# Sliding-window attention in half blocks of two heads x 64 queries, with its steps spread over more places

## The chip, the cores and the metric

The kernel runs on one core of a Trainium2 chip. A core has TensorE (PE; its weight loads are shown apart as PEld), VectorE (DVE), ScalarE (ACT), GpSimd (POOL) and SyncE (SP, which issues the DMAs). They run side by side and wait for each other through semaphores. The metric is the time of one execution on the device in microseconds (us).

## The reference

Two layers over 1024 positions of width 1024. Each layer mixes tokens, then channels. What the change touches is the windowed attention: 8 query heads of 64, 2 key/value heads (4 query heads share one), blocks of 128 queries that see their own block of keys and the one before, window 128, and a learned sink per head in the softmax.

```python
k_cat = jnp.concatenate([jnp.pad(kb, pad)[:, :-1], kb], axis=2)
v_cat = jnp.concatenate([jnp.pad(vb, pad)[:, :-1], vb], axis=2)
scores = jnp.einsum("bnqkgd,bnskd->bnkgqs", qb, k_cat).astype(jnp.float32)
scores = scores * (HEAD_DIM ** -0.5)
qi = jnp.arange(BLOCK)[:, None]
kj = jnp.arange(2 * BLOCK)[None, :]
diff = qi + BLOCK - kj
valid = (diff[None] >= 0) & (diff[None] < WINDOW) & (key_abs >= 0)
scores = jnp.where(valid[None, :, None, None], scores, NEG_INF)
probs = jax.nn.softmax(jnp.concatenate([scores, sink], axis=-1), axis=-1)[..., :-1]
out = jnp.einsum("bnkgqs,bnskd->bnqkgd", probs.astype(v.dtype), v_cat)
```

A query sees 128 keys; over a block of 128 queries they spread over 256 keys, over 64 queries over 191.

The rest of a layer: an input projection to q, k, v and a pooling branch, an output projection, a gated feed-forward net of inner width 2816, norms with modulation from a second input, and residuals.

## The kernel before

**Precision.** Dense factors are split into a high part, rounded to float32r, and a low rest (`split`, L213: ScalarE writes the high part at L215, VectorE subtracts at L216). A product of two such factors is three matmuls, high x high, high x low, low x high (`mm3`, L254: L255, L258, L259).

**Halves and streams.** The sequence is cut into 2 halves of 512 positions (`NHALF`), each into 4 blocks of 128 (`NT`). The program is written as generators. `run` (L640) drives one dense stream and, after each of its steps, as many steps of side streams as keep them in proportion; the compiler then orders each engine's instructions within what dependences and buffers allow. Half 0's attention runs beside the input projections of half 1 (`dense`, L1397); half 1's beside the output projection of half 0 (`mix_out`, L967, 16 steps, side stream: modulation sums, L289), then beside the pooling branch's projection (10 steps), then beside the first feed-forward products.

**Attention before.** A group is one block and one key/value head with its 4 query heads: 8 groups a half. A group takes four steps: (a) `att_keys` (each second group) and `att_queries`: keys and queries, high and low parts stacked, are transposed by TensorE (L774, L798) and copied by ScalarE (L784, L787, L803); (b) `att_softmax` of the group before; (c) and (d), for two heads each, `att_scores` (L813, L814: four matmuls with 256 keys; L816: scaling, mask and row maximum on VectorE), then the value products of the pair transposed in the step before, then `att_probs`: four transposes of probabilities (L851) and their split into `pth` and `ph`. In softmax, L835 is the exponential and L841 and L843 scale three rows on VectorE and one on ScalarE. `att_values` makes six matmuls of 256 columns per pair (current and previous block), whose stationary operand holds the 64 value columns of one head and 64 of zeros; all groups of a block add up in the one PSUM bank `pv`, which L879 copies out.

**Buffers.** A tag has a fixed number of buffers in rotation (L100 to L106); a tile that is asked for when all are in use waits for the oldest one's last reader. `msc` is three PSUM banks that attention, transposes and modulation share; `acc` is four banks of the dense products. The biased projections go to `qkv` (L696, L707): 4 tiles a half, 6 buffers.

## Time and profile before

| | us |
|---|---|
| median of 3 runs | 1915.66 |
| lowest, highest | 1914.08, 1919.38 |
| the profiled execution | 1912.51 |
| its span, first to last instruction | 1910.7 |

Granted TensorE clock: 0.997. A row of the groups reads: line, engine, operation, what it writes and reads, shapes (partitions x elements), count | busy us, mean ns of one | idle time of the engine just before, and who ended it. A row of the windows gives, for each engine, the busy time within the stretch and the count. A row of the timeline gives start, duration, engine, line and operation; neighbours of one kind are merged into one row with a count. [...]

### The profile page before, as it was taken

What the parts mean: (1) busy time and instruction counts of PE and PEld (TensorE: products, weight loads), DVE (VectorE), ACT (ScalarE), POOL (GpSimd) and SP (SyncE); (2) the same over time, 40 slices, a digit from 0 to 9 for tenths busy, and PEclk for the clock granted to TensorE, in tenths of its full rate; (3) what the DMA queues carried; (4) which work ended last, traced back from release to release, by engine and by line L of the source; (5) the groups of instructions that cost most, each with busy time, mean ns of one, the idle gap of its engine ahead of it and who ended that gap; (6) DMA issues with size and microseconds to landing.
All of it is one profiled execution on the core that took longest, in us unless ns stands there. A gap on an engine that the chain in (4) does not pass through costs nothing.

```text
span 1910.7 us, 26084 instructions
## 1 busy us (share of the span) xinstructions
PE 1866.3 (98%) x8978; PEld 1539.2 (81%) x8978; DVE 1545.1 (81%) x2898; ACT 950.5 (50%) x1789; POOL 26.8 (1%) x84
## 2 busy tenths in 40 slices
PE   6999999999999999999999989999999999999997
PEld 4887788888888888888888868888888887888886
DVE  5999886668898888788879998846889888877687
ACT  4876795653222223445548667845622222244452
POOL 1000000000000000000000000000000000000000
PEclk9999999999999999999999999999999999999999
DMA  9355563555655665944554464536654565574342
GB/s 324 115 155 153 163 226 122 186 177 183 204 179 189 208 207 178 323 137 145 183 168 128 133 183 165 177 110 208 215 188 150 198 209 202 197 252 150 115 152 102
DMA packets 227428, 341.86 MB, mean 179 GB/s; under 512 B 16952, under 2 KB 124360, under 8 KB 227296
## 3 DMA queue, kind: packets, MB, share of 16 engines
q1 hardware_dynamic: 227152, 340.17, 54.2%
q8 instruction: 70, 1.15, 0.2%
q14 instruction: 62, 0.51, 0.1%
q0 software_dynamic: 32, 0.00, 0.0%
q10 hardware_dynamic: 112, 0.04, 0.0%
HBM read 267.25 MB, written 72.89 MB: 178 GB/s over the span
## 4 chain that ended last, share of the span: by engine, by line
PE 79%; DVE 11%; DMA 5%; ACT 3%; issue 1%; SPq 0%; DVEq 0%; ACTq 0%
PE acc L255 24%; PE acc L258 24%; PE acc L259 24%; DMA ar<-in_ada_w_dram 2%; DVE lo L216 2%; DVE ada L289 2%; PE msc L851 1%; PE msc L519 1%; ACT hi L215 1%; DMA raw<-in_w_up_dram 1%; PE pv L255 1%; DVE ph L216 1%; DMA ar<-x 1%; DVE sb L816 1%; PE pv L258 1%
## 5 line engine op out<-in xcount | busy, mean ns | idle before, releaser
L215 ACT ACTIVATE hi<-raw 128x1024 fp32r<-128x1024 f32 (+1 forms) x388 | 332.4, 869 | 365.8 <-PE acc L258 196.2
L216 DVE TENSOR_TENSOR lo<-raw,hi 128x1024 fp32r<-128x1024 f32 (+1 forms) x388 | 380.0, 986 | 123.6 <-ACT hi L215 122.8
L255 PE MATMUL acc<-t,hi 128*128 128x512 f32 x704 | 274.6, 390 | 1.5 <-ACT hi L215 1.5
L258 PE MATMUL acc<-t,hi 128*128 128x512 f32 x704 | 274.0, 389 | 0.0
L259 PE MATMUL acc<-t,lo 128*128 128x512 f32 x704 | 271.9, 389 | 0.0
L255 PE MATMUL acc<-bh,hi 128*128 128x512 f32 x520 | 202.8, 390 | 0.0
L259 PE MATMUL acc<-bh,lo 128*128 128x512 f32 x520 | 202.4, 389 | 0.0
L255 PE MATMUL acc<-hT,hi 128*128 128x512 f32 x480 | 189.7, 395 | 0.6 <-DVE fn L638 0.6
L258 PE MATMUL acc<-hT,hi 128*128 128x512 f32 x480 | 188.4, 392 | 0.0
L259 PE MATMUL acc<-hT,lo 128*128 128x512 f32 x480 | 187.7, 392 | 0.0
L1107 DVE TENSOR_TENSOR fn<-acc,fn 128x512 f32<-128x512 f32 x220 | 150.2, 683 | 37.4 <-PE acc L259 37.4
L255 PEld LDWEIGHTS acc<-t,hi 128*128 128x128 f32 x704 | 132.2, 188 | 30.8 <-ACT hi L215 3.9
L259 PEld LDWEIGHTS acc<-t,lo 128*128 128x128 f32 x704 | 132.2, 188 | 29.0 <-DVE lo L216 1.5
L258 PEld LDWEIGHTS acc<-t,hi 128*128 128x128 f32 x704 | 132.2, 188 | 27.2
L258 PE MATMUL acc<-ph,hi 128*128 128x512 f32 x320 | 124.6, 389 | 0.0
L1043 ACT ACTIVATE fn<-fn 128x512 f32<-128x512 f32 x44 | 27.8, 633 | 180.3 <-DVE fn L1107 180.3
L289 DVE SCALAR_TENSOR_TENSOR ada<-ar,c_act,ada 128x512 f32<-128x512 f32 x140 | 104.6, 747 | 12.0 <-DMA ar<-in_ada_w_dram 11.0
L259 PEld LDWEIGHTS acc<-bh,lo 128*128 128x128 f32 x520 | 97.6, 188 | 20.4
L255 PEld LDWEIGHTS acc<-bh,hi 128*128 128x128 f32 x520 | 97.6, 188 | 20.0
L255 PEld LDWEIGHTS acc<-hT,hi 128*128 128x128 f32 x480 | 90.2, 188 | 18.9 <-DVE fn L638 1.4
L259 PEld LDWEIGHTS acc<-hT,lo 128*128 128x128 f32 x480 | 90.1, 188 | 18.2
L255 PE MATMUL acc<-hi 128*128 128x512 f32 x256 | 101.1, 400 | 2.8 <-DVE fn L638 1.6
(315 smaller groups left out, 3834.6 us busy)
## 6 DMA issues: line engine op xcount, KB each, us to landing
ar<-in_ada_w_dram SPq DMA_DIRECT2D x160, 256.0 KB
raw<-in_w_gate_dram SPq DMA_DIRECT2D x44, 512.0 KB
raw<-in_w_up_dram SPq DMA_DIRECT2D x44, 512.0 KB
raw<-in_w_in_dram SPq DMA_DIRECT2D x80, 256.0 KB
raw<-keeps SPq DMA_DIRECT2D x40, 512.0 KB
keeps<-fn SPq DMA_DIRECT2D x66, 256.0 KB
two_b<-in_w_down_dram SPq DMA_DIRECT2D x30, 512.0 KB
raw<-keepa SPq DMA_DIRECT2D x25, 512.0 KB
```

The lines of the kernel that those rows point to most:

```text
L215: nc.scalar.activation(hi, src, AF.Copy)
L216: recent["split"] = nc.vector.tensor_sub(lo, src, hi.bitcast(F32))
L255: ins = nc.tensor.matmul(dst, lh, rh, start=first, stop=False)
L258: nc.tensor.matmul(dst, lh, rl, start=False, stop=False)
L259: return nc.tensor.matmul(dst, ll, rh, start=False, stop=last)
L289: ins = nc.vector.scalar_tensor_tensor(acc, w, c_act[:, i : i + 1], acc, op0=ALU.mult, op1=ALU.add)
L519: ins = nc.tensor.transpose(bank[:, t * P : (t + 1) * P], src[t], ident)
L816: nc.vector.tensor_tensor_reduce(out=s[:, ii, :], in0=bank[:, ii * 2 * P : (ii + 1) * 2 * P], in1=mask[:, min(blk, 1), :], scale=SCALE, sc ...
L851: nc.tensor.transpose(bank[:, i * P : (i + 1) * P], s[:, ii, ck * P : (ck + 1) * P], ident)
L1043: nc.scalar.activation(g, g, AF.Silu)
L1107: nc.vector.tensor_add(halves_of(dst)[m], bank, halves_of(src)[m])
```

## The change

Scores are made for two heads x 64 queries in place of one head x 128: 64 queries see 192 keys at most (`SPAN`), so a score product has 192 columns and softmax rows are 192 wide. A group is now (block, r): query half h meets key/value head `h ^ r`, so that each group holds both halves and both heads. The probabilities of a pair lie in 384 columns, cut in three chunks of 128: the first belongs to half 0, the last to half 1, the middle one to both. The outer chunks meet V of the previous and of the current block, the middle one meets `mix`, a tile that takes 64 rows of each. So a group has three value products of three matmuls each in place of four, and six transposes in place of eight. In a layer's first block the absent past is left out. Values are written once per block into two tiles whose zeros are written once per layer (`att_room`).

The steps of a group now lie so: (a) the middle chunk's transposes of group g-2, queries of head 1; (b) keys of the next block, softmax of group g-1; (c) scores, value products of group g-2, V of this block; (d) scores, queries of head 0 of the next block, outer transposes of group g-1. The tail is one group longer (37 steps for 34). `qkv` has 5 buffers, `pth` one of 768 columns in place of two of 512, `qT` two, `vz` two wide ones. Tiles of `uT` and `pt` are given 576 columns, of which the same ones as before are used.

The diff, without the mask's new shape and the renamed widths:

```diff
+UW = 576
+QH = P // 2
+SPAN = P + QH
...
-        mix=dict(cfa=2, cfb=2, qkv=6, bqkv=1, uT=4, pt=2, vz=5, rt=1, qT=1, pth=2, pwh=1, pwl=1),
+        mix=dict(cfa=2, cfb=2, qkv=5, bqkv=1, uT=4, pt=2, vz=2, rt=1, qT=2, pth=1, bd=1, pwh=1, pwl=1),
...
+    def att_room():
+        attn["v"] = [t_("vz", [P, 2, 3, HD], F32R) for _ in range(2)]
+        attn["mix"] = t_("bd", [P, 2, 4, HD], F32R)
+        zero = vz_zero.rearrange("p (a d) -> p a d", a=1)
+        for v in attn["v"]:
+            nc.gpsimd.tensor_copy(v[:, :, 1, :], zero.to_broadcast([P, 2, HD]))
+        for i in range(4):
+            nc.gpsimd.tensor_copy(attn["mix"][:, :, i, :], zero.to_broadcast([P, 2, HD]))
+    def att_vals(blk, qkv):
+        v, mix = attn["v"][blk % 2], attn["mix"]
+        vsrc = qkv[:, QK:QKV].rearrange("p (n d) -> p n d", d=HD)
+        nc.scalar.activation(v[:, 0, 0:3:2, :], vsrc, AF.Copy)
+        nc.vector.tensor_sub(v[:, 1, 0:3:2, :], vsrc, v[:, 0, 0:3:2, :].bitcast(F32))
+        if blk:
+            before = attn["v"][1 - blk % 2]
+            nc.scalar.activation(mix[QH:, :, 0:4:3, :], before[QH:, :, 0:3:2, :].bitcast(F32), AF.Copy)
+        for n in range(NKV):
+            nc.scalar.activation(mix[:QH, :, 2 - n, :], v[:QH, :, 2 * n, :].bitcast(F32), AF.Copy)
     def att_keys(blk, qkv):
...
         stk = part("hi").rearrange("p (n o d) -> p n o d", n=NKV, o=4)
...
                 )
         bv = bank.rearrange("p (n o k) -> p (n o) k", n=NKV, o=2)
         if blk == 0:
...
+            attn["k", 0] = t_("sa", [P, NKV * 2, 2 * P], F32R)
         nc.scalar.activation(attn["k", blk][:, :, P : 2 * P], bv, AF.Copy)
         if blk + 1 < NB:
             nxt = t_("sa", [P, NKV * 2, 2 * P], F32R)
...
                 stk[:, i].rearrange("p a d -> p (a d)"), ident_r,
             )
         qT = t_("qT", [P, GRP * P], F32R)
-        nc.scalar.activation(qT, bank, AF.Copy)
+        nc.scalar.activation(
+            qT.rearrange("p (h i q) -> p h i q", h=2, i=GRP),
+            bank.rearrange("p (i h q) -> p h i q", h=2, i=GRP), AF.Copy,
+        )
         return qT
-    def att_scores(blk, n, u, qT, mx, s):
+    def att_seen(blk, h):
+        return slice((P if h == 0 else QH) if blk == 0 else 0, SPAN)
+    def att_scores(blk, r, u, qTs, mx, s):
         kT = attn["k", blk]
         bank = msc_bank()
...
+        for h in range(2):
+            n, cs = h ^ r, att_seen(blk, h)
+            dst = bank[:, h * SPAN : (h + 1) * SPAN][:, cs]
+            q = qTs[n][:, (2 * h + u) * P : (2 * h + u + 1) * P]
+            for o in range(2):
+                keys = kT[:, 2 * n + o, h * QH : h * QH + SPAN][:, cs]
+                nc.tensor.matmul(dst, q, keys, start=o == 0, stop=o == 1)
+        for h in range(2):
+            cs = att_seen(blk, h)
             nc.vector.tensor_tensor_reduce(
...
+                out=s[:, h * SPAN : (h + 1) * SPAN][:, cs], in0=bank[:, h * SPAN : (h + 1) * SPAN][:, cs],
+                in1=mask[:, cs], scale=SCALE, scalar=-3.0e38, op0=ALU.add, op1=ALU.max,
+                accum_out=mx[:, 2 * h + u : 2 * h + u + 1],
             )
+        if blk == 0:
+            nc.gpsimd.memset(s[:, 0:P], 0.0)
+            nc.gpsimd.memset(s[:, SPAN : SPAN + QH], 0.0)
         return s
-    def att_softmax(n, sts, mx, nsink):
-        hs = slice(n * GRP, (n + 1) * GRP)
+    def att_softmax(blk, r, sts, mx, nsink):
+        hs = slice(2 * r, 2 * r + GRP)
...
+        rows = [
+            sts[i % 2][:, i // 2 * SPAN : (i // 2 + 1) * SPAN][:, att_seen(blk, i // 2)] for i in range(GRP)
+        ]
         for i in range(GRP):
-            sl = sts[i // 2][:, i % 2, :]
-            nc.scalar.activation(sl, sl, AF.Exp, bias=nm[:, i : i + 1], accum_out=sm[:, i : i + 1])
+            nc.scalar.activation(rows[i], rows[i], AF.Exp, bias=nm[:, i : i + 1], accum_out=sm[:, i : i + 1])
         nc.vector.tensor_add(es, es, sm)
         nc.vector.reciprocal(es, es)
         for i in range(GRP):
-            sl = sts[i // 2][:, i % 2, :]
             if i < GRP - 1:
-                nc.vector.tensor_scalar(sl, sl, es[:, i : i + 1], None, op0=ALU.mult)
+                nc.vector.tensor_scalar(rows[i], rows[i], es[:, i : i + 1], None, op0=ALU.mult)
             else:
-                nc.scalar.activation(sl, sl, AF.Copy, scale=es[:, i : i + 1])
-    def att_probs(s):
+                nc.scalar.activation(rows[i], rows[i], AF.Copy, scale=es[:, i : i + 1])
+    def att_probs(blk, sts, ends, probs):
         bank = msc_bank()
...
+        chunks = ([0] if blk else []) + [2] if ends else [1]
+        for i in chunks:
+            for u in range(2):
+                at = (i + u) * P
+                nc.tensor.transpose(bank[:, at : at + P], sts[u][:, i * P : (i + 1) * P], ident)
+        cs = slice(chunks[0] * P, (chunks[-1] + 2) * P)
+        to = slice(0, 2 * P) if not ends else slice(chunks[0] * P, 4 * P)
+        split(*(p[:, to] for p in probs), bank[:, cs])
+    def att_values(blk, r, probs, pmid, cat, t):
+        if r == 0:
             attn["pv"] = ps.tile([P, 512], F32, tag="pv", name="pv", bufs=1)
         pv = attn["pv"]
...
+        v, before = attn["v"][blk % 2], attn["v"][1 - blk % 2]
+        at = 2 * (1 - r)
+        parts = [(before, r, probs, 0)] if blk else []
+        parts += [(v, 1 - r, probs, 2 * P), (attn["mix"], at, pmid, 0)]
+        for k, (src, c, (ph, pl), p0) in enumerate(parts):
+            vh, vl = (src[:, j, c : c + 2, :].rearrange("p a d -> p (a d)") for j in range(2))
+            opening, closing = r == 0 and k == 0, r == 1 and k == len(parts) - 1
             ins = mm3(
...
+                pv[:, r * 2 * P : (r + 1) * 2 * P], vh, vl, ph[:, p0 : p0 + 2 * P], pl[:, p0 : p0 + 2 * P],
+                opening, closing, None if opening else attn["open"],
             )
             if opening:
                 attn["open"] = ins
         if closing:
...
+            for n in range(NKV):
+                ns = slice(n * HD, (n + 1) * HD)
+                for h in range(2):
+                    g = h ^ n
+                    nc.scalar.activation(
+                        cat[ns, :, t * P + h * QH : t * P + (h + 1) * QH],
+                        pv[ns, g * 2 * P : (g + 1) * 2 * P].rearrange("p (j q) -> p j q", j=GRP), AF.Copy,
+                    )
+    ATT_STEPS = NT * 2 * 4 + 4
+    def attention(half, qkvs, nsink, cat):
+        NG = NT * 2
+        prev, late = None, None
+        for g in range(NG + 2):
             cur = None
+            if late:
+                pblk, pr, psts, probs, pmid, pcat, pt = late
+                att_probs(pblk, psts, False, pmid)
             if g < NG:
...
+                t, r = divmod(g, 2)
+                blk = half * NT + t
+                if g == 0:
+                    att_rotary(blk, qkvs[t])
                     att_keys(blk, qkvs[t])
+                    first = att_queries(0, qkvs[t])
+                if r == 0:
+                    qTs = [first, att_queries(1, qkvs[t])]
                     if t + 1 < NT:
                         att_rotary(blk + 1, qkvs[t + 1])
...
+                both = t_("sb", [P, GRP // 2, 2 * SPAN])
+                cur = (blk, t, r, [], t_("st", [P, 8]))
+            if cur or late:
                 yield
+            if cur and r == 1 and t + 1 < NT:
+                att_keys(blk + 1, qkvs[t + 1])
+            nxt = None
             if prev:
-                pblk, pt, pn, sts, mx = prev
-                att_softmax(pn, sts, mx, nsink)
+                pblk, pt, pr, sts, mx = prev
+                att_softmax(pblk, pr, sts, mx, nsink)
+                pth = t_("pth", [P, 3 * 2 * P], F32R)
+                probs = pth[:, : 4 * P], t_("ph", [P, 4 * P], F32R)
+                pmid = pth[:, 4 * P :], t_("ph", [P, 4 * P], F32R)[:, : 2 * P]
+                nxt = pblk, pr, sts, probs, pmid, cat, pt
                 yield
...
+            if cur:
+                cur[3].append(att_scores(blk, r, 0, qTs, cur[4], both[:, 0]))
+            if late:
+                pblk, pr, _, probs, pmid, pcat, pt = late
+                att_values(pblk, pr, probs, pmid, pcat, pt)
+            if cur and r == 1:
+                att_vals(blk, qkvs[t])
+            if cur or late:
                 yield
-            prev = cur
-        flush()
+            if cur:
+                cur[3].append(att_scores(blk, r, 1, qTs, cur[4], both[:, 1]))
+                if r == 1 and t + 1 < NT:
+                    first = att_queries(0, qkvs[t + 1])
+            if nxt:
+                att_probs(nxt[0], nxt[2], True, nxt[3])
+            if cur or nxt:
+                yield
+            prev, late = cur, nxt
...
         bq = t_("bqkv", [P, QKV])
         eng = nc.sync
         eng.dma_start(bq, b_in[l : l + 1, 0:QKV].to_broadcast([P, QKV]))
+        each = t_("st", [P, 8])
+        eng.dma_start(each, sinks[l : l + 1, :].to_broadcast([P, NH]))
         sk = t_("sk", [P, NH])
-        eng.dma_start(sk, sinks[l : l + 1, :].to_broadcast([P, NH]))
-        nc.vector.tensor_scalar(sk, sk, -1.0, None, op0=ALU.mult)
+        for i in range(2):
+            rows = slice(i * QH, (i + 1) * QH)
+            src = each[rows].rearrange("p (m i) -> p m i", i=2)[:, :, i]
+            nc.vector.tensor_scalar(sk[rows, 0:4], src, -1.0, None, op0=ALU.mult)
+            nc.vector.tensor_scalar(sk[rows, 4:6], src[:, 0:2], -1.0, None, op0=ALU.mult)
         d["bq"], d["nsink"] = bq, sk
...
         run(dense0(), 12 if l else 4, (side, 2 if l else 1))
         cats[0] = (t_("cfa", [P, 4, T]), t_("cfa", [P, 4, T]))
         qkvs[1] = [t_("qkv", [P, QKV]) for _ in range(NT)]
+        att_room()
         att = attention(0, qkvs[0], par["nsink"], cats[0][0])
```

92 lines of the change are left out of this document (9 added, 83 removed).

## The prediction

> **What bounds the kernel now.** I read the page first (busy shares), then the windows of the stages in which attention runs, then the timeline for the real pace of TensorE, because the page's busy time is modelled.
>
> ```profile
> span 1910.7 us, 26084 instructions
> PE 1866.3 (98%) x8978; PEld 1539.2 (81%) x8978; DVE 1545.1 (81%) x2898; ACT 950.5 (50%) x1789; POOL 26.8 (1%) x84
> PE 79%; DVE 11%; DMA 5%; ACT 3%; issue 1%; SPq 0%; DVEq 0%; ACTq 0%
> ...
> core 0: us, PE busy (x) PEld busy (x) DVE busy (x) ACT busy (x) POOL busy (x), PEclk, DMA share, GB/s
> 65.00:163.00 98.00, 97.44 (x620) 83.75 (x618) 93.44 (x280) 77.51 (x191) 2.40 (x12) 1.00 0.43 125
> 163.00:201.00 38.00, 33.31 (x166) 24.94 (x165) 36.11 (x92) 23.37 (x56) 0.39 (x2) 1.00 0.65 186
> 201.00:270.00 69.00, 67.12 (x381) 55.53 (x380) 57.63 (x173) 58.19 (x146) 2.89 (x8) 1.00 0.58 194
> 1100.00:1140.00 40.00, 34.52 (x166) 26.10 (x165) 37.04 (x96) 25.14 (x60) 0.00 (x0) 0.97 0.64 182
> ```
>
> The chain is TensorE's for 79%. In layer 0, half 0's attention lies in 65 to 163, half 1's in 163 to 201 (beside the output projection) and 201 to 270. TensorE sets the first and third stretch; in the second VectorE is 95% busy (36.11 of 38) and TensorE waits, as in layer 1's 1100 to 1140 (37.04 of 40). So TensorE work taken out of attention shortens the kernel, provided VectorE loses as much in that second stretch.
>
> The pace of TensorE, from the timeline:
>
> ```profile
> 86.71 0.28 PE L255 MATMUL pv<-pth,vz 128*128 128x256 f32 x1
> 86.83 0.28 PE L258 MATMUL pv<-ph,vz 128*128 128x256 f32 x1
> 86.95 0.28 PE L259 MATMUL pv<-pth,vz 128*128 128x256 f32 x1
> 87.07 0.49 PE L851 MATMUL msc<-ident,sb 128*128 128x128 f32 x3
> 92.86 0.39 PE L255 MATMUL acc<-hT,hi 128*128 128x512 f32 x1
> 93.09 0.39 PE L258 MATMUL acc<-hT,hi 128*128 128x512 f32 x1
> ...
> L851 PE MATMUL msc<-ident,sb 128*128 128x128 f32 x256 | 43.7, 277 | 4.0 <-DVE sb L841 3.0 <-ACT raw L512 0.6 <-DVE st L816 0.3
> 788.18 0.86 PEld L416 LDWEIGHTS msc<-ones_r,ada 128*128 128x128 f32 x7
> L416 PEld LDWEIGHTS msc<-ones_r,ada 128*128 128x128 f32 x32 | 4.2, 191 | 0.3
> L814 PEld LDWEIGHTS msc<-sa,qT 128*128 128x128 f32 x128 | 24.3, 190 | 1.4
> ```
>
> A product of 256 columns lasts 0.28 us but starts 0.12 after the one before it; one of 512 starts 0.23 after. Three probability transposes last 0.49 together, one alone 0.277, so they start 0.11 apart. L416 streams one column, so its seven weight loads show the pace of loading alone: (0.86 - 0.19) / 6 = 0.11 us. The score products' loads last as long (190 ns), so I take 0.11 us as the floor of a product, however few columns it has.
>
> **The change part by part.** There are 16 blocks (8 per layer); 14 are ordinary, and 2 are the first of a layer.
>
> TensorE, per ordinary block. Value products fall from 24 to 18, all still 256 wide: 6 x 0.12 = 0.72 us. Probability transposes fall from 16 to 12: 4 x 0.11 = 0.44. The 16 score products shrink from 256 to 192 columns; with the floor that is 16 x (0.12 - 0.11) = 0.16. Bounds: 0 if a product of 192 keeps the pace of 256, and 0.43 if it shrinks in proportion ((0.23 - 0.12) / 256 = 0.43 ns a column, 64 columns, 16 products); its nearest row is the load floor. Together 1.32 us, 18.5 for 14 blocks. First blocks drop the past: value products 24 to 12 (1.44), transposes 16 to 8 (0.88), scores 0.16, so 2.48, twice 5.0. TensorE loses **23.5 us**. Key and query transposes keep their number.
>
> [...] I follow the trace's load floor.
>
> VectorE and ScalarE:
>
> ```profile
> L816 DVE CUSTOM_DVE_ANT_0 sb<-msc,mask 128x256 f32<-128x256 f32 x128 | 50.4, 416 | 6.0 <-PE msc L814 5.6
> L216 DVE TENSOR_TENSOR ph<-msc,pth 128x512 fp32r<-128x512 f32 x64 | 43.7, 686 | 2.6 <-ACT pth L215 2.0
> L841 DVE TENSOR_SCALAR sb<-sb,st 128x256 f32<-128x256 f32 x45 | 13.2, 347 | 0.2
> L795 DVE TENSOR_TENSOR hi<-qkv,hi 128x256 fp32r<-128x256 f32 x16 | 6.7, 420 | 0.1
> L501 DVE TENSOR_SCALAR cfb<-cfb,rs 128x1024 f32<-128x1024 f32 x2 | 1.4, 745 | 0.0
> L756 DVE TENSOR_TENSOR vz<-qkv,vz 128x64 fp32r<-128x64 f32 x16 | 3.3, 231 | 2.0 <-PE pv L258 2.0
> L835 ACT ACTIVATE sb<-sb,st 128x256 f32<-128x256 f32 x128 | 63.7, 506 | 6.3 <-DVE st L828 6.3
> L215 ACT ACTIVATE pth<-msc 128x512 fp32r<-128x512 f32 x64 | 37.8, 597 | 22.0 <-PE msc L851 21.8
> L794 ACT ACTIVATE hi<-qkv 128x256 fp32r<-128x256 f32 x32 | 13.2, 412 | 5.7 <-PE acc L259 4.9 <-DVE ada L289 0.8
> L755 ACT ACTIVATE vz<-qkv 128x64 fp32r<-128x64 f32 x16 | 3.4, 250 | 6.1 <-DVE qkv L696 4.4 <-PE pv L259 1.7
> L879 ACT ACTIVATE cfa<-pv 128x512 f32<-128x512 f32 x4 | 2.3, 584 | 0.0
> L392 ACT ACTIVATE ar<-msc 4x512 f32<-4x512 f32 x1 | 0.6, 589 | 0.6 <-PE msc L388 0.6
> ```
>
> VectorE's slope is (686 - 420) / 256 = 1.04 ns a column, and (745 - 347) / 768 = 0.52 for the scaling of L841. Per ordinary block: 8 mask reductions shorter by 64 columns, 8 x 66 = 0.53 us; 6 scalings, 0.20; two of four low halves of 512 become 256 wide, 2 x 266 = 0.53; the V low halves become one of two, 231 against some 300 instead of 462, 0.16. That is 1.42, 20 us for 14 blocks and, with narrower rows and no past, some 3 for each first block: about **26 us**. In the VectorE-bound stretch run 16 of half 1's 37 steps (1.7 blocks a layer): VectorE saves 1.42 a block where TensorE would have saved 1.32, so that stretch shortens as much and the 23.5 stands.
>
> ScalarE gains work. Its slope is (597 - 412) / 256 = 0.72 ns a column. One copy of the finished block (584 ns) becomes four of 64 partitions x 256, which cost like 128 x 256, since 4 partitions (L392) cost 589; 4 x 412 - 584 = +1.06 us. The mixed V tile adds one copy of 256 columns and two of 128, 412 + 2 x 300 = +1.01. Less: 8 exponentials x 46, one scaling, two shorter high halves of 185, and one V copy instead of two (0.2): -1.0. Net **+1.1 us a block**, 17 in all. I cost it at nothing: ScalarE is 58.19 of 69 busy even from 201 to 270, where 2.3 blocks bring 2.5 us. If that cover fails it costs up to 2.5 a layer.
>
> GpSimd loses the zeroing of keys and of each block's V, and gains six zero copies per layer and two memsets per score pair in the first block; it is busy 1% of the span, so zero, except that first-block transposes wait for a memset. SP sees one small load under another tile name; attention issues no DMA.
>
> The placement. Softmax, transposes and value products now lie two steps apart where one lay between them, the second query transposes run one step before the scores, and keys run a step earlier. That could remove at most these idles:
>
> ```profile
>   ACT pth L215: 7.4, 18
>   DVE sb L841: 4.0, 9
> ```
>
> 11.4 us of TensorE idle, before the value products and before the transposes; where VectorE is full, what comes late next is the low half or a weight's split, so I take 3 of it. Against it stand new waits. V copies wait for the last block's value products, as today (L756, 2.0). The value bank is free only after four copies, 1.65 us for 0.58, with a step between. With one pth buffer for two, ScalarE's high half waits for the previous group's value products; behind it on ScalarE lie the splits of dense weights, and TensorE waits for those. With 5 qkv buffers for 6, the last bias add of half 1's keys (L696) waits for block 2's V copies:
>
> ```profile
> 123.81 0.60 ACT L879 ACTIVATE cfa<-pv 128x512 f32<-128x512 f32 x1
> 125.35 0.74 DVE L696 TENSOR_TENSOR qkv<-acc,bqkv 128x256 f32<-128x256 f32 x2
> ```
>
> Block 1's values close at 123.81, block 2's V is split right after them, and the adds come at 125.35: about 1.5 us to spare. Behind the add on VectorE lie weight splits, and TensorE's query pass waits for its bank. I take 3 us in all for new waits, bounds 0 and 12 (the sum of today's idles before attention again); they cancel the 3 gained.
>
> Sum: the profiled execution took 1912.51 us (span 1910.7). 1912.5 - 23.5 = 1889.0. The median of the runs, 1915.66, lies 3.2 above it, so the same change counted from there gives 1892; I forecast **1890**; its own range, with the score bounds (2.6 less, 6 more) and half the bound on waits, is 1880 to 1900.
>
> **The rivals.**
>
> *Narrow float32r products leave the fast pace* (slower). No row shows a float32r product under 256 columns except transposes:
>
> ```profile
> 89.39 0.46 PE L798 MATMUL msc<-ident,hi 128*128 128x128 f32 x4
> 18.97 0.08 PEld L355 LDWEIGHTS msc<-cfa,c_act 128*1 128x1 f32 x1 [0.34 <-issue]
> 19.40 0.08 PEld L355 LDWEIGHTS msc<-cfa,c_act 128*1 128x1 f32 x1 [0.34 <-issue]
> L355 PE MATMUL msc<-cfa,c_act 128*1 128x512 f32 x16 | 9.4, 752 | 6.7 <-DMA cfa<-in_ada_w_dram 6.7
> ```
>
> L355 is plain float32: 8 products leave 16 records 0.43 apart, so 0.86 us for 512 columns, four times the float32r pace. At that pace a score product of 192 takes 0.32, 0.20 more than now: 14 x 16 x 0.20 = 45 us, about 1 more in first blocks, and the 2.6 counted for scores goes: 1889 + 49 = **1938**. It decides from about 0.21 us per product ((23.5 - 2.6) / 224 above 0.12). For it: 256 is the narrowest product in the trace. Against it: four L798 transposes of 128 columns take 0.46, under 0.1 apart, though a transpose may be treated apart. Chance 0.13. [...]
>
> *New waits eat the gain.* ScalarE's 17 us and the shorter buffer rings show on the path: 12 of waits and 5 of ScalarE gives 1889 + 17 = **1906**. For it: three engines are over 79% busy in 65 to 163. Against it: all values wait longer before use. Chance 0.14.
>
> *More than the forecast.* Scores shrink in proportion (6 us more, first blocks included) and 7 of the 11.4 of idle go too: **1876**. Chance 0.10.
>
> *The change does not do what it says*: a place one step off may leave the engines' order as it was, since dense products fill the same time. Then only counts act, and 23.5 stands: 1889, inside the forecast.
>
> **How the numbers follow.** Forecast 0.63, more 0.10, waits 0.14, narrow products 0.13. The range 1872 to 1912 holds the first two and most of the third. A measurement of this kernel tells about 0.3% (6 us) from no change: faster means under 1910. Faster is 0.63 + 0.10 + 0.07; the same 0.06; slower 0.14.
>
> **What would show it.** Right: 92 value products on each of L255, L258 and L259 in place of 128, 184 transposes in place of 256, score products of 192 columns starting 0.11 apart, mask reductions near 350 ns, VectorE still full in the output projection but that stretch some 2 us shorter. Wrong: score products over 0.2 us apart; TensorE idle before value products or L255 behind a pth or V copy on ScalarE; a late L696.

## The result and the profile after

| | before | after |
|---|---|---|
| median, us | 1914.87 (4 runs) | 1933.12 (4 runs) |
| lowest, highest | 1913.30, 1919.38 | 1928.87, 1936.38 |
| the profiled execution | 1912.51 | 1928.87 |
| its span | 1910.7 | 1927.1 |

The ratio is 1.0093, with a 95% interval of 1.0071 to 1.0114: the changed kernel is 0.9% slower, where 1890 us and faster was forecast. Lines have moved: `split` is L220 and L221, `mm3` is L260, L263, L264, the key copies are L795 and L798, the query transposes L809, the scores L836, the mask reductions L839, the scalings on VectorE L868, the probability transposes L883, the copies of the value bank L912.

The page of the changed kernel: the busy time of each engine, and the shares of the chain that ended last.

```profile
span 1927.1 us, 25753 instructions
PE 1853.1 (96%) x8798; PEld 1525.9 (79%) x8798; DVE 1525.3 (79%) x2888; ACT 959.6 (50%) x1871; POOL 18.7 (1%) x65
PE 73%; DVE 12%; ACT 8%; DMA 5%; issue 2%; SPq 0%; DVEq 0%; ACTq 0%
```

TensorE has 180 instructions less, as counted in the prediction, and less work: with each matmul put in at the start-to-start distance of its form (0.227 us for 512 columns, 0.119 for 256, 0.113 for 192, 0.08 to 0.10 for transposes) the sum is 1829.0 us before and 1807.4 after. That is 21.6 less, beside the 23.5 of the prediction. But the span grew by 16.4. So TensorE stands idle, or runs slowly, for 120 us in place of 82, and its share of the chain falls from 79% to 73%.

Where the idle time is shows in the windows. First the changed kernel, in two of the stretches that the prediction used:

```profile
core 0: us, PE busy (x) PEld busy (x) DVE busy (x) ACT busy (x) POOL busy (x), PEclk, DMA share, GB/s
65.00:163.00 98.00, 90.93 (x564) 77.26 (x563) 87.55 (x274) 76.22 (x209) 1.82 (x6) 0.99 0.44 133
163.00:201.00 38.00, 31.73 (x143) 25.27 (x142) 33.37 (x92) 20.76 (x50) 0.00 (x0) 0.90 0.59 166
```

Beside the input projections TensorE was busy 97.44 of 98 us before and is 90.93 now, with 564 matmuls for 620; VectorE and ScalarE do not fill the gap (87.55 for 93.44 and 76.22 for 77.51). No engine is the bound there. The engines wait for each other. In the second stretch VectorE is at 33.37 of 38 where it was at 36.11, so it isn't the bound any more either, and the granted clock is 0.90.

What TensorE waits for, from the view of waits (total us, times, longest), changed kernel:

```profile
PE msc L809 <- DVE st L839: 6.6, 5, 2.6
PE msc L836 <- DVE st L839: 4.7, 3, 2.9
PE msc L260 <- DVE st L839: 3.1, 3, 1.6
PE msc L883 <- DVE st L839: 1.5, 1, 1.5
```

Four kinds of users of an `msc` bank wait for L839: the mask reduction, which frees the bank of a score pair. They sum to 15.9 us. The timeline shows one such wait (start, duration, engine, line; in brackets the idle time before and what ended it):

```profile
120.05 0.59 PE L836 MATMUL msc<-sa,qT 128*128 128x192 f32 x4
...
121.57 0.59 PE L836 MATMUL msc<-sa,qT 128*128 128x192 f32 x4
...
121.64 0.78 DVE L868 TENSOR_SCALAR sb<-sb,st 128x192 f32<-128x192 f32 x3
...
122.33 1.08 DVE L701 TENSOR_TENSOR qkv<-acc,bqkv 128x256 f32<-128x256 f32 x3
...
123.33 0.35 DVE L839 CUSTOM_DVE_ANT_0 sb<-msc,mask 128x192 f32<-128x192 f32 x1
...
124.02 0.54 PE L809 MATMUL msc<-ident,hi 128*128 128x128 f32 x4 [1.86 <-DVE st L839]
```

The first four score products end at 120.64. VectorE has other work ahead of their mask reduction, at the end scalings and bias adds, and comes to it at 123.33, 2.7 us later; the next query transposes wait for the bank until 124.02. The score products themselves are not slow: four last 0.59 in all, and their median distance is 0.113 us.

### The profile page after: what moved, and what is told of

It reads as the page before. It is cut to its first block, busy times and chain, and to the rows that moved or that the text cites. A ratio compares the mean times of both kernels' runs of the same rounds, so it can differ in the third digit from the quotient of the medians.

```text
span 1927.1 us, 25753 instructions
## 1 busy us (share of the span) xinstructions
PE 1853.1 (96%) x8798; PEld 1525.9 (79%) x8798; DVE 1525.3 (79%) x2888; ACT 959.6 (50%) x1871; POOL 18.7 (1%) x65
## 4 chain that ended last, share of the span: by engine, by line
PE 73%; DVE 12%; ACT 8%; DMA 5%; issue 2%; SPq 0%; DVEq 0%; ACTq 0%
PE acc L260 23%; PE acc L264 23%; PE acc L263 23%; DVE lo L221 2%; DMA ar<-in_ada_w_dram 2%; DVE ada L294 2%; DMA raw<-in_w_up_dram 1%; ACT sb L863 1%; ACT hi L220 1%; PE msc L524 1%; DVE ph L221 1%; ACT junk L481 1%; DVE sb L839 1%; DMA h<-raw 1%; ACT pth L220 1%
## 5 line engine op out<-in xcount | busy, mean ns | idle before, releaser
L220 ACT ACTIVATE hi<-raw 128x1024 fp32r<-128x1024 f32 (+1 forms) x388 | 332.5, 869 | 371.8 <-PE acc L263 200.5
L221 DVE TENSOR_TENSOR lo<-raw,hi 128x1024 fp32r<-128x1024 f32 (+1 forms) x388 | 380.5, 987 | 131.5 <-ACT hi L220 128.4
L260 PE MATMUL acc<-t,hi 128*128 128x512 f32 x704 | 274.6, 390 | 2.8 <-ACT hi L220 2.8
L263 PE MATMUL acc<-t,hi 128*128 128x512 f32 x704 | 274.0, 389 | 0.0
L264 PE MATMUL acc<-t,lo 128*128 128x512 f32 x704 | 271.9, 389 | 0.0
L260 PE MATMUL acc<-bh,hi 128*128 128x512 f32 x520 | 202.9, 390 | 0.0
L264 PE MATMUL acc<-bh,lo 128*128 128x512 f32 x520 | 202.4, 389 | 0.0
L260 PE MATMUL acc<-hT,hi 128*128 128x512 f32 x480 | 192.8, 402 | 4.0 <-ACT uT L726 2.5
L263 PE MATMUL acc<-hT,hi 128*128 128x512 f32 x480 | 189.2, 394 | 0.0
L264 PE MATMUL acc<-hT,lo 128*128 128x512 f32 x480 | 188.7, 393 | 0.0
L260 PEld LDWEIGHTS acc<-t,hi 128*128 128x128 f32 x704 | 132.1, 188 | 32.2 <-ACT hi L220 5.2
L264 PEld LDWEIGHTS acc<-t,lo 128*128 128x128 f32 x704 | 132.1, 188 | 29.3 <-DVE lo L221 1.8
L263 PEld LDWEIGHTS acc<-t,hi 128*128 128x128 f32 x704 | 132.1, 188 | 27.2
L263 PE MATMUL acc<-ph,hi 128*128 128x512 f32 x320 | 124.7, 390 | 0.0
L260 PEld LDWEIGHTS acc<-bh,hi 128*128 128x128 f32 x520 | 97.6, 188 | 20.6 <-ACT sb L1255 0.4
L264 PEld LDWEIGHTS acc<-bh,lo 128*128 128x128 f32 x520 | 97.6, 188 | 20.5
L260 PEld LDWEIGHTS acc<-hT,hi 128*128 128x128 f32 x480 | 91.0, 190 | 22.7 <-DVE fn L643 3.1
L264 PEld LDWEIGHTS acc<-hT,lo 128*128 128x128 f32 x480 | 90.7, 189 | 19.2 <-DVE lo L221 0.3
L263 PEld LDWEIGHTS acc<-hT,hi 128*128 128x128 f32 x480 | 91.2, 190 | 16.3
```

What stands on the lines that cost most here:

```text
L220: nc.scalar.activation(hi, src, AF.Copy)
L221: recent["split"] = nc.vector.tensor_sub(lo, src, hi.bitcast(F32))
L260: ins = nc.tensor.matmul(dst, lh, rh, start=first, stop=False)
L263: nc.tensor.matmul(dst, lh, rl, start=False, stop=False)
L264: return nc.tensor.matmul(dst, ll, rh, start=False, stop=last)
```

## The experiments

All times are medians; the ratio is to runs of the kernel before on the same chip, with its 95% interval. The kernel before has medians of 1913.6 to 1915.6 us on these chips, so small differences between runs of different chips are better read from the ratios. A letter of a theory is explained where it first stands; only B has another meaning in the runs on PSUM banks (e11, e14) than in the first four.

| run | us | ratio |
|---|---|---|
| e1_key_bank_free | 1930.94 | 1.0088 [1.0066, 1.0110] |
| e2_near | 1938.99 | 1.0125 [1.0110, 1.0141] |
| e3_full_keys_early | 1922.03 | 1.0044 [1.0029, 1.0059] |
| e4_scalar_light | 1926.20 | 1.0058 [1.0043, 1.0073] |
| e5_wide_scores | 1907.45 | 0.9968 [0.9955, 0.9982] |
| e6_near_wide | 1907.38 | 0.9968 [0.9958, 0.9978] |
| e7_full_252 | 1979.48 | 1.0342 [1.0323, 1.0362] |
| e8_full_256_control | 1921.11 | 1.0039 [1.0025, 1.0054] |
| e9_wide_mix_on_gpsimd | 1897.70 | 0.9912 [0.9895, 0.9928] |
| e10_wide_scalar_light | 1892.52 | 0.9891 [0.9876, 0.9905] |
| e11_wide_two_column_jobs | 1908.18 | 0.9977 [0.9959, 0.9996] |
| e14_before_two_column_jobs | 1919.91 | 1.0034 [1.0022, 1.0046] |
| e15_252_in_order_of_256 | 1919.44 | 1.0022 [1.0012, 1.0032] |
| e16_narrow_in_order_of_wide | 1907.56 | 0.9973 [0.9958, 0.9989] |
| e17_narrow_best | 1900.68 | 0.9930 [0.9908, 0.9951] |
| e18_wide_in_order_of_narrow | 1931.05 | 1.0089 [1.0069, 1.0110] |
| e19_light_in_order_of_wide | 1896.52 | 0.9896 [0.9873, 0.9920] |
| e20_gpsimd_in_order_of_wide | 1900.40 | 0.9921 [0.9902, 0.9941] |

### First: the bank, the places, ScalarE

In the changed kernel the second copy of a block's keys, L798, comes 4.5 to 9.8 us after the first, L795, in 10 of its 14 blocks (119.50 and 124.59 in one), because it waits for a free key tile; an `msc` bank is held so long. The first run lets that copy read the first one's result, so that the bank is free at once:

```diff
-            nc.scalar.activation(nxt[:, :, 0:P], bv, AF.Copy)
+            nc.scalar.activation(nxt[:, :, 0:P], attn["k", blk][:, :, P : 2 * P].bitcast(F32), AF.Copy)
```

> The changed kernel, with one edit: the second copy of the keys (into the next block's key tile) reads the first copy's tile in place of the PSUM bank, so the bank is free after the first copy. Theory A (keys, placed one step earlier, hold one of the three msc banks until the scores of the same group release the next key tile; 5 to 10 us between L795 and L798 in the changed trace against 0.5 before): most of the 35 to 40 us by which TensorE waits more than forecast goes, 1890 to 1910. Theory B (ScalarE's added copies are late) and theory C (the whole placement crowds the banks, five users in two neighbouring steps): 1925 to 1935, little changed.

1930.94 us: no gain that could be told from the changed kernel's 1933.12. The held key bank is not the cause.

The second run keeps the half blocks but puts the steps as near to their users as the kernel before had them:

```diff
             if late:
-                pblk, pr, psts, probs, pmid, pcat, pt = late
-                att_probs(pblk, psts, False, pmid)
+                pblk, pr, probs, pmid, pt = late
+                att_values(pblk, pr, probs, pmid, cat, pt)
...
+            for u in range(2):
+                if cur:
+                    cur[3].append(att_scores(blk, r, u, qTs, cur[4], both[:, u]))
+                if nxt:
+                    att_probs(pblk, sts, u == 0, nxt[2 + u])
```

> Half blocks as in the changed kernel, but the steps placed as near as before: keys and both queries at the start of a block, outer transposes with the first scores, middle ones with the second, value products at the next step, V of the block in its second group. Theory A and theory C: the loss goes, 1885 to 1905. Theory B, or half blocks being slow by themselves: 1925 to 1940.

1938.99 us, 5.9 more than the changed kernel. With narrow products the half blocks are slow at either placement, and the farther places win some 6 us of it back.

The third takes the kernel before and moves only its keys a step earlier, as the change does:

```diff
+            if cur and n == 1 and t + 1 < NT:
+                att_keys(blk + 1, qkvs[t + 1])
```

> The kernel before, full blocks, with one edit: the key part of att_keys for the next block is placed one step earlier, with the softmax of the block's second group, as in the change; V stays where it was. Theory A: the key bank is held there too, so the kernel becomes slower by 10 to 30 us, 1925 to 1945, with 5 us or more between the two key copies. Theories B and C: within 6 us of before.

1922.03 us, 7 more than before, which lies between the two ranges that were expected. This move costs the full blocks something, but it is no account of the whole, since the run above, without it, is slower still.

The fourth leaves out work that the change adds to ScalarE: the mixed V tile is not filled, and the finished value bank is copied at once into another layout, in place of four copies (`L912`).

```diff
-            nc.scalar.activation(mix[QH:, :, 0:4:3, :], before[QH:, :, 0:3:2, :].bitcast(F32), AF.Copy)
...
-                    nc.scalar.activation(
-                        cat[ns, :, t * P + h * QH : t * P + (h + 1) * QH],
-                        pv[ns, g * 2 * P : (g + 1) * 2 * P].rearrange("p (j q) -> p j q", j=GRP), AF.Copy,
-                    )
+            nc.scalar.activation(
+                cat[:, :, t * P : (t + 1) * P], pv.rearrange("p (j q) -> p j q", j=GRP), AF.Copy
+            )
```

> The changed kernel without the work that it adds on ScalarE: one copy of the finished block in place of four, and no copies into the mixed V tile (it stays zero, and the block's columns lie in the wrong order; all matmuls are kept). About 2 us of ScalarE less per block. Theory B: 1890 to 1905. Theories A and C: 1922 to 1935.

1926.20 us: 7 us of the 43 between forecast and result.

### The width of a score product

What was left is the score product itself. In the next two runs it is given 256 columns again, of which the mask reduction reads the same 192 as before (the first block's unused keys are zeroed by GpSimd); e6 has the near places of e2 besides.

```diff
-                keys = kT[:, 2 * n + o, h * QH : h * QH + SPAN][:, cs]
-                nc.tensor.matmul(dst, q, keys, start=o == 0, stop=o == 1)
+                nc.tensor.matmul(dst, q, kT[:, 2 * n + o, :], start=o == 0, stop=o == 1)
```

> The changed kernel with each score product 256 columns wide as before (all keys of two blocks; softmax reads the same 192 of them; in a layer's first block the absent keys are zeros again). Theory D (the compiler plans each engine's order with times of its own, and gives a float32r product under 256 columns far more than the 0.11 us it takes, so that the other engines' work is ordered for a TensorE that is later than the real one): although TensorE gets no less work, 1888 to 1905. Theory E (half blocks have a longer chain by themselves): 1925 to 1938.

> The half blocks with the near placement (as e2_near), and score products 256 columns wide. Theory D: 1885 to 1910, and the difference to e5_wide_scores is what the placement is worth. Theory E: 1930 to 1940.

1907.45 and 1907.38 us. Wider products make the kernel 26 us faster, although TensorE's sum rises from 1807.4 to 1808.9. For e5 that is 2.5 us above the range of theory D and far under that of E. And with wide products the places make no difference: near and far agree within 0.1 us.

The reverse was tried on the kernel before, in full blocks: score products of 252 columns, and as a control the same edits with 256. Both leave the first 4 keys of each span of 256 out of the softmax (GpSimd zeroes their probabilities).

```diff
-            dst = bank[:, ii * 2 * P : (ii + 1) * 2 * P]
+            dst = bank[:, ii * 2 * P + CUT : (ii + 1) * 2 * P]
...
-            nc.tensor.matmul(dst, q, kT[:, 2 * n, :], start=True, stop=False)
+            nc.tensor.matmul(dst, q, kT[:, 2 * n, CUT:], start=True, stop=False)
```

> The kernel before, full blocks, with score products of 252 columns: the first 4 keys of each pair of blocks are left out of scores and softmax, and their probabilities are set to zero. TensorE's work is the same within 0.3 us. Theory D: the order changes at under 256 columns, and the kernel becomes 8 to 30 us slower than e8_full_256_control. Theory E: the same as the control within 4 us.

> The control to e7_full_252: the same edits, 4 keys left out of mask, softmax and probabilities, but score products of all 256 columns. Both theories: 1910 to 1922, within 6 us of before.

1979.48 and 1921.11 us: four columns fewer cost 58 us, about twice the most that theory D expected. The products start 0.118 us apart in one and 0.119 in the other, and TensorE's sum is 1829 us in both. The windows, 252 columns first, then 256:

```profile
65.00:163.00 98.00, 83.44 (x529) 71.17 (x527) 83.90 (x246) 67.43 (x167) 5.87 (x24) 0.98 0.36 111
```

```profile
65.00:163.00 98.00, 97.45 (x617) 83.69 (x616) 93.50 (x281) 78.09 (x194) 4.20 (x30) 1.00 0.42 124
```

The sickness is that of the changed kernel, only stronger: 83.44 us of TensorE for 97.45. The waits in the 252 kernel:

```profile
PE pv L256 <- ACT pth L216: 13.1, 13, 3.6
PE msc L853 <- DVE sb L843: 12.2, 9, 2.8
PE pv L259 <- DVE ph L217: 9.6, 14, 2.0
PE acc L256 <- ACT hi L216: 8.9, 9, 2.7
```

What differs between the two programs besides the columns is the order that the compiler gave the instructions of an engine. A stretch of TensorE's order in half 0, read off the two programs (S score products, V value products, T probability transposes, Q query transposes, e products of 256 columns of the projections; the number is how many stand in a row):

```
252 columns:  e24  S4 V6 T4 S4 V6 T4  e24  Q4  e24  S4 V6 T4 S4 V6 T4
256 columns:  e22  S4 V6 e17 T1 S1 T3 S3 T3 V1 T1 e7 V5 Q4  e24  S4 V6
```

In this stretch, with 256, dense products stand between a step of attention and the step that needs its softmax. With 252 the steps stand together and the dense products in lumps.

### What is left of the forecast

With wide products the kernel lies 17 us above the forecast. The next runs took the added ScalarE work away again, now from the wide kernel: one puts the copies into the mixed V tile on GpSimd, the other leaves the work out as e4 did.

```diff
-            nc.scalar.activation(mix[QH:, :, 0:4:3, :], before[QH:, :, 0:3:2, :].bitcast(F32), AF.Copy)
+            nc.gpsimd.tensor_copy(mix[QH:, :, 0:4:3, :], before[QH:, :, 0:3:2, :].bitcast(F32))
         for n in range(NKV):
-            nc.scalar.activation(mix[:QH, :, 2 - n, :], v[:QH, :, 2 * n, :].bitcast(F32), AF.Copy)
+            nc.gpsimd.tensor_copy(mix[:QH, :, 2 - n, :], v[:QH, :, 2 * n, :].bitcast(F32))
```

> Wide score products (256 columns) with the V copies into the mixed tile put on GpSimd in place of ScalarE; the wide kernel alone took 1907.5 us. Theory S (the added ScalarE copies still cost part of the 17 us between 1907 and the forecast of 1890): ScalarE loses 8 x 4 to 5 copies per layer, about a third of what the run without any added copies saved, so 1903 to 1906. Rival (ScalarE's load is free once the products are wide, what is left is elsewhere): 1906 to 1909. Rival (GpSimd's copies are slow and late for the values): over 1912.

> Wide score products, and all the ScalarE copies that the change adds left out: no mixed V tile filled, one copy of the value bank in place of four. In the narrow kernel the same cut took 7 us. Theory S: 1907.5 - 7 = 1899 to 1903. Rival (with wide products ScalarE has room): 1906 to 1909. The forecast of 1890 would need 17 us from ScalarE alone.

1897.70 and 1892.52 us. Both lie under all the ranges that were expected of them. The first is the fastest kernel of the study that does all the work: 0.9912 of the time before. The second, without any of the added copies, comes within 2.5 us of the forecast of 1890. Its page:

```profile
span 1889.4 us, 25718 instructions
PE 1843.2 (98%) x8798; PEld 1518.6 (80%) x8798; DVE 1519.3 (80%) x2888; ACT 932.2 (49%) x1777; POOL 22.9 (1%) x73
```

ScalarE is busy 932.2 us where it is 958.9 in the wide kernel, 26.7 less, and the kernel takes 14.9 less. Whether that is ScalarE's load or again another order, these two runs don't say; the last two runs were made to part them.

Two more tested whether PSUM banks are short in general. A pair of modulation jobs holds an `msc` bank over four jobs; single jobs free it, in the wide kernel with the copies on GpSimd and, as a control, in the kernel before.

```diff
-        return ada_stream(ada_gate(l, 0) + ada_pair(l, 1, par["cols"], par["abf"]))
+        return ada_stream(ada_gate(l, 0) + ada_columns(l, 1, par["cols"], par["abf"]))
```

> The wide kernel with the V copies on GpSimd, and the second modulation of a layer computed by single column jobs in place of a pair that holds one PSUM bank over four jobs. Theory B (with three banks asked for by scores, queries, keys and modulation, a bank held so long makes TensorE wait for VectorE to free another): 5 to 10 us under the run with the V copies on GpSimd alone, 1895 to 1901. Rival (banks are not short once the order is good): within 3 us of that run.

> The kernel before with single column jobs in place of the pair, nothing else: the control for the run above. Theory B holds for half blocks alone if this stays at 1912 to 1918; if it also falls by 5 or more, the held bank costs the kernel before as much and says nothing of the change.

1908.18 us, 10.5 more than e9, and 1919.91, 6.3 more than before: neither lies in a range that was expected. Single jobs cost more than the freed bank brings, in both kernels. The theory of the held bank falls; whether the single jobs lose by their additional work or by another order wasn't separated.

### The order by itself

That the order changes with the width doesn't prove that the order costs the time. The next four runs part the two. The program is ordered once with products of one width; then products of the other width are built, and every instruction of TensorE, VectorE and ScalarE is tied behind the one that stood before it on its engine in that first order.

```diff
+        if plan is not None:
+            last = {}
+            for j in plan:
+                i = traced[j]
+                e = str(i.engine)
+                if e in last:
+                    tc.add_manual_dep(
+                        i, last[e].name,
+                        mybir.DependencyInfo(mybir.DependencyClass.NoSync, mybir.DependencyReason.DATA),
+                        reason="order",
+                    )
+                last[e] = i
```

> The products of 252 columns of the 1979 us run, with the instructions of TensorE, VectorE and ScalarE held in the order that the compiler chose for the products of 256 (the 1921 us run). Theory D (the width acts through the order alone): 1915 to 1925. Rival H (the chip itself runs products under 256 columns worse, in a way that the start times do not show): 1965 to 1985.

> The changed kernel's narrow products (192 columns, 128 to 192 in the first block), with the three engines held in the order chosen for the wide products (1907.5 us). Theory D: 1903 to 1909, the wide kernel's time or a microsecond or two under it. Rival H: 1925 to 1935, as the changed kernel.

> As the run above, and the V copies into the mixed tile on GpSimd, held in the order of that wide kernel (1897.7 us). Theory D: 1894 to 1899, and so under both kernels. Rival H: 1915 to 1925.

> The mirror: products of 256 columns, held in the order that the compiler chooses when they are narrow. Theory D: 1926 to 1938, the changed kernel's time although the products are wide. Rival H: 1904 to 1911, the wide kernel's.

All four go with the order, none with the width; only e17 lies outside the range of theory D, 1.7 us above it. Products of 252 in the order of 256 take 1919.44 us, not 1979.48 (e15, with the same 4 keys left out). The changed kernel's own narrow products in the wide order take 1907.56 (e16), and 1900.68 with the copies on GpSimd (e17). Wide products in the narrow order take 1931.05 (e18). The ties themselves cost nothing that shows: e16 takes as long as the wide kernel, whose order it has. Windows of e15, then of e18:

```profile
65.00:163.00 98.00, 97.50 (x622) 83.90 (x622) 93.84 (x281) 77.93 (x194) 4.23 (x30) 1.00 0.41 122
```

```profile
65.00:163.00 98.00, 89.85 (x559) 76.37 (x558) 86.67 (x272) 75.14 (x206) 1.82 (x6) 1.00 0.45 132
```

TensorE is full with products of 252 columns in the good order (97.50) and starved with wide products in the bad one (89.85). In e18 the wait of the timeline above is back at nearly the same place:

```profile
120.10 0.64 PE L844 MATMUL msc<-sa,qT 128*128 128x256 f32 x4
...
121.66 0.64 PE L844 MATMUL msc<-sa,qT 128*128 128x256 f32 x4
...
123.26 0.35 DVE L847 CUSTOM_DVE_ANT_0 sb<-msc,mask 128x192 f32<-128x192 f32 x1
...
124.05 0.51 PE L813 MATMUL msc<-ident,hi 128*128 128x128 f32 x4 [1.75 <-DVE st L847]
```

The view of waits says the same of the whole kernel. TensorE's waits for the mask reduction, 15.9 us in the changed kernel, follow the order and not the width. First e16 (narrow products, wide order), then e18 (wide products, narrow order); L847 is the mask reduction in both:

```profile
PE msc L261 <- DVE st L847: 1.7, 1, 1.7
PE msc L844 <- DVE st L847: 0.5, 1, 0.5
```

```profile
PE msc L844 <- DVE st L847: 4.5, 3, 2.1
PE msc L261 <- DVE st L847: 3.2, 4, 1.2
PE msc L813 <- DVE st L847: 2.4, 3, 1.7
PE msc L891 <- DVE st L847: 1.6, 1, 1.6
```

That is 2.2 and 11.7 us. In the kernel with 252 columns the order is bad in another way: there the longest waits are for the split probabilities and the scalings, as shown above.

One number tells the orders apart, though it doesn't give the size of the loss. From the end of the two products of one row block to the start of their mask reduction on VectorE, over the 64 first reductions of a pair, the median is:

| kernel | products | order chosen for | median, us | kernel, us |
|---|---|---|---|---|
| after | 192 | narrow | 1.79 | 1933.1 |
| e18 | 256 | narrow | 1.88 | 1931.1 |
| e16 | 192 | wide | 0.72 | 1907.6 |
| e5 | 256 | wide | 0.62 | 1907.5 |
| e7 | 252 | narrow | 1.80 | 1979.5 |
| e15 | 252 | wide | 0.89 | 1919.4 |
| e8 | 256 | wide | 0.85 | 1921.1 |

For narrow products the compiler puts about 1 us more of other VectorE work ahead of the reduction, as if it took the scores to be ready later than they are. Each score pair holds its `msc` bank, and each softmax starts, that much later. The delay alone is no measure of the loss: with nearly the same delay, e7 loses 58 us to its control and the changed kernel 26 to e16. Why the compiler reckons so was not tried; that it does so below 256 columns and not at 256 is shown for 252 and 192.

The same means settles ScalarE's copies: the kernels of e10 and e9, with all instructions that they share with the wide kernel of e5 held in its order. The copies that go are left out of the list.

```diff
+        for to, fro in pairs:
+            if PLANNING[0]:
+                DROP.add(nc.scalar.activation(to, fro, AF.Copy).ins.name)
...
+        traced = [i for i in bb.instructions if i.name not in DROP]
```

> The kernel without the added ScalarE copies (1892.5 us in an order of its own), now with the rest of the instructions of the three engines held in the order of the wide kernel that has them (1907.5 us). It leaves out the filling of the mixed V tile and puts the value bank into another layout with one copy. Theory S (the copies cost by their time on ScalarE, in front of splits that dense products wait for): 1890 to 1897. Rival O (leaving them out helped by changing the order once more): 1903 to 1908.

> The wide kernel with the copies into the mixed V tile on GpSimd (1897.7 us in an order of its own), with the rest held in the order of the wide kernel that has them on ScalarE (1907.5 us). Theory S: 1896 to 1901. Rival O: 1904 to 1909.

1896.52 us without the copies (the mixed V tile not filled, the value bank in another layout) and 1900.40 with part of them on GpSimd, in the order of the kernel that takes 1907.45. So by the medians 10.9 of the 14.9 us come from the copies themselves, and the 4.0 left may be order; by the ratios, 0.9968, 0.9896 and 0.9891, it is about 14 of 15, so that the part of the order is not told from nothing. For GpSimd it is 7.1 of 9.8, and the copies are still made there: that part is ScalarE's load. In e19 the value bank also comes free after one copy in place of four, which wasn't tested apart. So ScalarE, busy only 50% of the span of e5 (958.9 of 1904.2 us), still cost time there. The reason that theory S gave isn't borne out: TensorE's waits for ScalarE's high halves are not shorter, 5.1 us in e5 and 6.3 in e19. Its waits for the scaling are, 2.7 and 0.6, which is too little for the whole, so which waits make up the gain stays open. First e5, then e19:

```profile
PE acc L260 <- ACT hi L220: 5.1, 8, 1.0
PE msc L885 <- DVE sb L870: 2.7, 4, 1.1
```

```profile
PE acc L262 <- ACT hi L222: 6.3, 8, 1.1
PE msc L889 <- DVE sb L874: 0.6, 1, 0.6
```

## Why the prediction was wrong

**TensorE, −23.5 us: right.** 92 value products a line and 184 transposes, as counted; the sum by starts fell by 21.6. Narrow score products start 0.113 apart, on the floor of 0.11 that was taken from L416.

**VectorE, −26 us: the right kind, too large.** Its busy time fell by 19.8 (1545.1 to 1525.3). The mask reductions have a median of 352 ns, as forecast near 350. It made no difference: in the stretch from 163 to 201 VectorE has room now.

**The step that failed: the score products and the places.** The prediction priced the narrow score product only by TensorE's pace, "16 x (0.12 - 0.11) = 0.16", with bounds of 0 and 0.43 a block, and took the order of the engines as something that only the places could alter ("a place one step off may leave the engines' order as it was"). The width altered it. New waits were costed at 3 us with an upper bound of 12; the order that came with 192 columns costs 25.6 (1933.12 to 1907.56, with the same products in both; 23 by the ratios). The waits were named at the wrong place, too: the prediction looked at `pth`, the V copies and L696, and TensorE waits for the mask reduction: 15.9 us, of which the wide order leaves 2.2.

**The places themselves, 0: right with the wide order.** Far and near take 1907.45 and 1907.38. In the narrow order far is 5.9 better.

**ScalarE, costed at nothing: wrong.** The cover was given as ScalarE's room in the stretches of attention, and the price without it as "up to 2.5 a layer". Its busy time rose by only 9.1 (950.5 to 959.6, forecast 17). But with the order mended and held, leaving the added copies out saves 10.9, more than twice that price. The two are not the same amount of work: what was left out is some 27 us of ScalarE, what was priced is a rise of 17.

The sum: 1890 was forecast; 1892.5 is measured without the added copies and with wide products, in that kernel's own order (e10). The copies cost 10.9 and what may be the order that comes with them 4.0, which gives 1907.4; the order of the narrow products is 25.6, which gives 1933. That e10 comes so near to 1890 is partly luck: it leaves out work that the change needs, and its ScalarE is busy 932.2 us, 18 less than in the kernel before, where the forecast counted 17 more.

**The rivals.** "Narrow float32r products leave the fast pace" named the right edit and, with 1938, nearly the time, by a mechanism that isn't there: the products keep the fast pace (0.113 us apart at 192 columns, 0.119 at 256). Its test, starts over 0.2 us apart, would have missed the cause. "New waits eat the gain", 1906, is what the change is worth once the order is mended (1907.6): there it was right, and in part for its reason, ScalarE's work on the path, though ScalarE's part was put at 5 and is 10.9. "The change doesn't do what it says" had the order unchanged; the opposite came.

## What to carry to other kernels

Where a compiler orders the instructions, an edit of a shape can also be an edit of the order on every engine: before a smaller product is counted as a gain, compare the orders of the two programs, and after it look at how long the users of a result stand from its producer. When the time gets worse although TensorE and VectorE have less to do, as here, the order is a suspect; the test is to hold one program's order while the other's shapes run. Here the narrow products gain nothing, even in the wide order, and the wide form with the V copies on GpSimd is the kernel to keep: 1897.70 us, 0.9912 [0.9895, 0.9928] of the time before.

## What the hardware showed that was not expected

In the changed kernel some of TensorE's idle time was paid for twice: after it the granted clock fell to 0.50 for a while. The timeline, matmuls alone:

```profile
160.07 0.39 PE L392 MATMUL msc<-ph,picks 128*4 128x512 f32 x1 [1.52 <-ACT ph L220]
160.79 0.40 PE L393 MATMUL msc<-ph,picks 128*4 128x512 f32 x1 [0.33 <-DVE ph L221]
...
161.55 0.63 PE L263 MATMUL acc<-lo,hT 128*128 128x512 f32 x1
...
163.68 0.63 PE L260 MATMUL acc<-hi,hT 128*128 128x512 f32 x1
164.11 0.63 PE L263 MATMUL acc<-lo,hT 128*128 128x512 f32 x1
164.54 0.53 PE L264 MATMUL acc<-hi,hT 128*128 128x512 f32 x1
164.91 0.39 PE L260 MATMUL acc<-hi,hT 128*128 128x512 f32 x1
165.13 0.40 PE L263 MATMUL acc<-lo,hT 128*128 128x512 f32 x1
```

After waits of 1.52 and 0.33 us, products of 512 columns start 0.43 us apart from 161.55 to 164.54, and 0.23 apart from 164.91 on. Its windows of 20 us show the clock:

```profile
160.00:180.00 20.00, 17.34 (x72) 13.82 (x73) 17.62 (x47) 10.06 (x25) 0.00 (x0) 0.83 0.45 122
...
280.00:300.00 20.00, 15.83 (x74) 13.10 (x73) 13.19 (x40) 14.35 (x34) 0.00 (x0) 0.83 0.46 138
```

The trace also records when the granted clock was at 0.50. Leaving the last 8 us of each kernel aside, that is seven stretches in the changed kernel, five of 3.4 us and two of 6.8; a wait of TensorE of 1.43 to 2.94 us ended 0.7 to 2.1 us before each. The one stretch in the kernel before, from 1137.96, follows waits of 0.77 and 0.79 us, and after the wait of 1.86 us that ends at 124.02 in the changed kernel there is none, so these traces show no length of wait that decides it. In these stretches, the products of 512 columns that start 0.30 to 0.48 us apart exceed 0.227 us by 8.2 us in all in the changed kernel, 1.2 in the kernel before, 8.7 in e7 and 4.1 in e16. So about 4 of the 19.4 us between the profiled executions of the changed kernel (1928.87) and of e16 (1909.44) are the clock's, as an estimate from these distances.
